# A gated DeltaNet and RWKV-7 decoder block: a rewritten bundle of stages, triangular solves whose joins are held in place, six product steps per RWKV chunk, and the decay products in quarters

## The chip, the cores and the metric

The kernel runs on one core of a Trainium2 chip. The metric is device time in microseconds of one execution, as the median of several. The engines are TensorE (PE in the profile, with its weight loads as PEld), VectorE (DVE), ScalarE (ACT), GpSimd (POOL) and SyncE (SP), which issues the transfers. Each engine runs its instructions in program order; they wait for each other by semaphores.

## The reference

One decoder block on 512 tokens of width 1024, all in float32. In short:

```
mod = silu(c) @ w_ada + b_ada                      # six vectors: shift, scale, gate twice
h   = rms_norm(x) * (1 + scale1) + shift1
p   = h @ w_in                                     # q, k, v, z, gates, the RWKV inputs, ga, gb
q, k, v = silu(causal_conv4(qkv)); q, k l2-normalised per head
# DeltaNet, 8 heads of 64, chunks of 64 tokens:
decay = exp(g_cum[i] - g_cum[j]) for i >= j
T   = inverse(I + strict_lower((beta k) k^T * decay))
o   = chunked recurrence with T, q k^T * decay, state S
y_a = rms_norm(o) * silu(z)
# RWKV-7, 8 heads of 64: S_t = S diag(decay_t) + (S a_t) b_t^T + v_t k_t^T; y_t = S_t r_t
y_b = (group_norm(y) + bonus) * g
x   = x + gate1 * ((sigmoid(ga) * (y_a @ w_bg) + sigmoid(gb) * (y_b @ w_br)) @ w_out)
h   = rms_norm(x) * (1 + scale2) + shift2
x   = x + gate2 * (silu(causal_conv3(h @ w_gate)) * (h @ w_up)) @ w_fo
out = rms_norm(x)
```

The kernel computes the RWKV recurrence in chunks of 64 as well, so both mixers need the inverse of many unit triangular 64x64 matrices (8 heads x 8 chunks each).

## The kernel before, in words

Everything is kept transposed: features on the 128 partitions, the 512 tokens along the free axis. A weight tile of 128 output columns is loaded whole (1024 rows, 512 KB), and split into a high and a low part in fp32r: ACT rounds (whi, L146) and DVE subtracts (wlo, L149). One **step** of a product is three 128x128 by 128x512 matmuls (high x high, high x low, low x high; mm3, L187, L190 and L191), and 8 steps make an output tile of the input projection. The first seven output tiles are made together, one k at a time, straight behind the norm (first_tiles, L310): for each k DVE computes two entries of mod (ada, L202), ACT and DVE make the normalised input (norm_h), and the weights are split on POOL.

All other products stand in a queue. A generator (stream, L232) works it off; fill(n) lets it emit n steps, need(label) lets it run until a product is done. The code between these calls is the rest of the block, and so fill is how steps of products are put into the gaps of the dependent parts. The remaining entries of mod are made by half reductions on DVE (ada_half, L211), some ahead of each product (its late number); their one buffer (wada) is reloaded by SP for each. Instructions are then ordered by a scheduler, which keeps each engine's order free of needless waits by its own estimate; where last["hold"] is set, mm3 gets a dependency on the last small matmul that was emitted through step (L182), so that the products stay where fill put them.

The parts in order:

- first tiles, then convolution and SiLU of q and k, the gates (beta, and the log decay gl, L445 to L478);
- l2 norm of q and k (l2norm, L481), then for each of four groups of two chunks the decay: gt = gl x a triangular mask (POOL, L505), a product with tri_gt (L509), its exponential and mask (DVE, L512), and a product with ones_x (L517) for the total decay eg;
- the chunk products k k^T and q k^T (L622), multiplied by the decay on DVE (L623, L627) and POOL (L624);
- the solve (L541): the 32x32 diagonal blocks are written to a spill buffer (L548) and read back with one matrix per partition (L551), DVE turns and negates them (L552), POOL masks (L553), and 30 elimination steps of two operations (L559, L561) invert them. The inverses go back through two more spill buffers (L563 to L573; ACT turns one copy, L565). After the yield come the joins: four groups of 32 small products (L582, L592) that make the off-diagonal blocks, with ACT's evacuations (L587, L597) between them;
- between the solve and its joins: q and k turned to natural layout (to_natural, L604 and L607), the products of v and the first RWKV inputs, the decay LoRA (L675);
- the DeltaNet scan over 8 chunks (five steps of the stream a chunk, hold set), with the preparation of RWKV among its gaps;
- the RWKV chunk products (L807), the second solve, the output norm (L825) and the first branch product, which the joins of the second solve follow;
- the RWKV scan (L856), 8 steps of the stream a chunk (3, 3 and 2, at L864, L870 and L895);
- group norm, the second branch with the merge (L936), w_out with the residual (L959), and the channel mixer (first_tiles again, L1010, and 37 + 8 products).

Of the kernel before, what the change touches and what calls it, by code (L numbers as in the profile page):

```python
# [18 lines left out]
ALU = mybir.AluOpType  # L19
# [36 lines left out]
def body(ctx, tc, io, out, tap=lambda name, ap: None):  # L56
# [143 lines left out]
    def ada(j, w):  # L200
        sp.dma_start(w, io["w_ada"][j])
# [24 lines left out]
    def product(label, src, xs_, evac, psum=mm, late=0, halves=False, spare=None):  # L226
# [3 lines left out]
        return dict(label=label, pieces=pieces, n=n, xs=xs_, evac=evac, psum=psum, late=late, halves=halves)  # L230

    def stream():  # L232
        while queue:
            it = queue.pop(0)
            for _ in range(min(it["late"], len(ada_rest))):
                ada_half(*ada_rest.pop(0))
# [73 lines left out]
    def first_tiles(src, count, banks, xs_, ready, side, cut=False, behind=()):  # L310
        for k in range(KT):
            ready(k)
            raw = raw_tile()
            sp.dma_start(raw[:, :128 * count].rearrange("p (n j) -> p n j", n=count),
                         src[0:count].rearrange("n p j -> p n j")[:, :, k * 128:(k + 1) * 128])
            hi = wp.tile([128, 1024], F32R, name="whi", tag="whi", bufs=2)
            lo = wp.tile([128, 1024], F32R, name="wlo", tag="wlo", bufs=2)
            split(hi[:, :128 * count], lo[:, :128 * count], raw[:, :128 * count], side if k else dve, () if k else behind)
# [14 lines left out]
    cond = const.tile([128, D], F32, name="cond")  # L333
    table(EXP)
    fn(sc_, cc, AF.Exp, scale=-1.0)
    dve.tensor_scalar(sc_, sc_, 1.0, None, op0=ALU.add)
    dve.reciprocal(sc_, sc_)
    dve.tensor_tensor(sc_, sc_, cc, op=ALU.mult)
    pool.affine_select(out=diag.rearrange("p (k t) -> p k t", k=KT), in_=sc_.unsqueeze(2).broadcast_to([128, KT, 128]),
                       pattern=[[0, KT], [-1, 128]], base=0, channel_multiplier=1, compare_op=ALU.is_equal, fill=0.0)  # L340
    for u in range(2):
        p = pc()
        pe.matmul(p, one, diag[:, T * u:T * u + T], start=True, stop=True)
        act.copy(cond[:, T * u:T * u + T], p)
# [16 lines left out]

    def first_h(k):
        w = slot((2, 3, 8, 9, 12)[k]) if k < 5 else slot2((0, 2, 1)[k - 5])
        ada(8 + k, w[:, 0:D])
        ada(k, w[:, D:2 * D])
        dve.scalar_tensor_tensor(A1[:, k:k + 1], mod[:, 8 + k:9 + k], 1.0, col("norm1", k),
                                 op0=ALU.add, op1=ALU.mult)
        made.append(norm_h(hh[k], hl[k], xT(k), rstd, A1[:, k:k + 1], mod[:, k:k + 1]))

    first_tiles(io["w_in"], 7, first_ps, hx, first_h, pool, behind=whole)  # L370
    sp.dma_start(cons, io["cons"])

    def inproj(t, evac, psum=mm):
        queue.append(product(t, io["w_in"][t], hx, evac, psum, late=2 if t >= T_GB else 2 if t >= T_GA else 0 if t >= T_Z else 0))
# [785 lines left out]
```

## Time and profile before

| what | us |
|---|---|
| median of 3 runs (lowest, highest) | 943.73 (942.07, 944.73) |
| the profiled execution, its own time | 943.86 |
| its span, first to last instruction | 942.2 |
| mean granted TensorE clock | 0.970 |
| first tiles | 16.1 to 65.3 |
| conv, gates, decay, chunk products | 65.3 to 120.7 |
| DeltaNet solve until its joins end | 120.9 to 208.7 |
| DeltaNet scan | 208.7 to 286.3 |
| RWKV chunk products, second solve, its joins | 286.3 to 385.4 |
| RWKV scan | 385.4 to 455.5 |
| group norm | 455.5 to 484.0 |
| merge and w_out | 484.0 to 565 |
| channel mixer | 565 to 942.2 |

The difference of 1.7 between time and span lies around the span. A row of the timeline gives start, duration, engine, line, operation, output <- inputs, shape, and in brackets the idle time before it with what ended it; "xN" means N records in a row. A row of the groups gives count | busy time, mean ns | idle time before it and what ended most of it. L numbers are those of the kernel before.

### The profile page before, as it was taken

The page shows a single profiled execution, that of the slowest core. Times are in us where ns is not written, and L with a number is a line of the kernel's source. Part 1 is how long each engine was busy: PE and PEld are TensorE (multiplying, and loading weights), DVE is VectorE, ACT ScalarE, POOL GpSimd, SP SyncE. Part 2 cuts the span into 40 slices and gives each one's busy share as a digit, 9 for nine tenths or more (in the row PEclk, how much of TensorE's full clock was granted, in tenths as well). Part 3 has the DMA queues.
Part 4 walks back from the last instruction along what each step waited for, and adds up shares of the span by engine and source line. Part 5 has one row for each costly group of instructions (what it writes and reads, how often), then busy time and mean ns, then how long its engine had stood idle before and what let it go on. Part 6 is the DMA issues. An engine that isn't in the chain of part 4 may idle for free.

```text
span 942.2 us, 13945 instructions
## 1 busy us (share of the span) xinstructions
PE 887.0 (94%) x5463; PEld 690.9 (73%) x5463; DVE 548.0 (58%) x865; ACT 413.5 (44%) x663; POOL 150.0 (16%) x126
## 2 busy tenths in 40 slices
PE   5989889989989998899999999999999999999996
PEld 3666566876666776777667788888888888888885
DVE  7988988934976684245568537464544544322233
ACT  5247535355537658323465425343333333332231
POOL 2334630001542100011232230000000000010112
PEclk7999989989999999799999999999999999999998
DMA  9741232473234577444567543332232233533322
GB/s 322 261 151 46 67 101 68 144 170 102 58 90 112 197 232 202 142 146 153 186 200 256 181 139 91 106 106 96 90 103 99 89 105 97 173 101 100 96 89 90
DMA packets 81696, 126.26 MB, mean 134 GB/s; under 512 B 26237, under 2 KB 43005, under 8 KB 81566
## 3 DMA queue, kind: packets, MB, share of 16 engines
q1 hardware_dynamic: 81630, 125.36, 42.4%
q8 instruction: 43, 0.70, 0.3%
q14 instruction: 23, 0.19, 0.1%
HBM read 110.14 MB, written 14.68 MB: 132 GB/s over the span
## 4 chain that ended last, share of the span: by engine, by line
PE 70%; DVE 14%; ACT 7%; DMA 3%; issue 3%; POOL 2%; SPq 0%; DVEq 0%; ACTq 0%; POOLq 0%
PE ps_mm L187 19%; PE ps_mm L191 19%; PE ps_mm L190 19%; PE ps_pc L182 3%; DVE wlo L149 2%; ACT whi L146 1%; DVE slot L202 1%; ACT slot L607 1%; DMA wada<-in_w_ada 1%; DVE slotd L202 1%; DVE wada L211 1%; PE ps_pa L592 1%; ACT tmp_rs L94 1%; PE ps_pc L187 1%; PE ps_pa L622 1%
## 5 line engine op out<-in xcount | busy, mean ns | idle before, releaser
L187 PE MATMUL ps_mm<-hh,whi 128*128 128x512 f32 (+1 forms) x714 | 292.1, 410 | 8.5 <-ACT hh L306 3.5
L191 PE MATMUL ps_mm<-hh,wlo 128*128 128x512 f32 (+1 forms) x714 | 282.5, 396 | 4.7 <-POOL wlo L149 3.5
L190 PE MATMUL ps_mm<-hl,whi 128*128 128x512 f32 (+1 forms) x714 | 282.3, 395 | 1.5 <-DVE hl L307 1.5
L149 DVE TENSOR_TENSOR wlo<-raw,whi 128x1024 fp32r<-128x1024 f32 (+2 forms) x133 | 156.7, 1178 | 169.1 <-ACT whi L146 163.5
L146 ACT CAST whi<-raw 128x1024 fp32r<-128x1024 f32 (+2 forms) x140 | 136.9, 979 | 242.8 <-PE ps_mm L190 190.4
L187 PEld LDWEIGHTS ps_mm<-hh,whi 128*128 128x128 f32 x714 | 136.0, 191 | 47.6 <-issue 9.8
L191 PEld LDWEIGHTS ps_mm<-hh,wlo 128*128 128x128 f32 x714 | 136.6, 191 | 37.9 <-POOL wlo L149 5.2
L190 PEld LDWEIGHTS ps_mm<-hl,whi 128*128 128x128 f32 x714 | 136.7, 191 | 32.1 <-issue 3.6
L191 PE MATMUL ps_mm<-slot,wlo 128*128 128x512 f32 (+1 forms) x154 | 58.5, 380 | 1.7 <-DVE wlo L149 1.7
L187 PE MATMUL ps_mm<-slot,whi 128*128 128x512 f32 (+1 forms) x154 | 58.0, 379 | 0.0
L190 PE MATMUL ps_mm<-slot,whi 128*128 128x512 f32 (+1 forms) x122 | 45.4, 372 | 0.0
L968 POOL COPY tmp_rs<-tmp_sq 128x512 f32<-128x512 f32 x2 | 2.1, 1066 | 268.8 <-ACT tmp_sq L965 268.8
L211 DVE CUSTOM_DVE_ANT_0 wada<-wada,cond,cols 128x512 f32<-128x512 f32 x32 | 25.1, 785 | 26.5 <-DMA wada<-in_w_ada 26.3
L211 DVE CUSTOM_DVE_ANT_0 wada<-wada,cond,half 128x512 f32<-128x512 f32 x32 | 25.2, 787 | 21.7 <-DMA wada<-in_w_ada 21.6
L187 PE MATMUL ps_mm<-slotd,whi 128*128 128x512 f32 (+1 forms) x96 | 36.4, 379 | 0.0
L190 PE MATMUL ps_mm<-slotd,whi 128*128 128x512 f32 (+1 forms) x96 | 36.1, 376 | 0.0
L191 PE MATMUL ps_mm<-slotd,wlo 128*128 128x512 f32 (+1 forms) x96 | 36.1, 376 | 0.0
L970 POOL TENSOR_TENSOR tmp_rs<-tmp_rs,tmp_sq 128x512 f32<-128x512 f32 x12 | 19.5, 1624 | 103.8 <-ACT tmp_sq L965 103.8
L191 PEld LDWEIGHTS ps_mm<-slot,wlo 128*128 128x128 f32 x154 | 29.0, 188 | 9.1 <-DVE wlo L149 4.0
L1035 DVE TENSOR_TENSOR tmp_sg<-tmp_acc,ps_mm 128x512 f32<-128x512 f32 x20 | 13.8, 688 | 35.6 <-PE ps_mm L191 35.5
L385 DVE SCALAR_TENSOR_TENSOR tmp_acc<-ps_mm,cols,tmp_acc 128x511 f32<-128x511 f32 (+2 forms) x44 | 32.8, 745 | 0.7
L187 PEld LDWEIGHTS ps_mm<-slot,whi 128*128 128x128 f32 x154 | 28.9, 188 | 5.8 <-ACT whi L146 0.4
(279 smaller groups left out, 1336.0 us busy)
## 6 DMA issues: line engine op xcount, KB each, us to landing
raw<-in_w_in SPq DMA_DIRECT2D x40, 512.0 KB, 3.5
raw<-in_w_fi SPq DMA_DIRECT2D x37, 512.0 KB, 3.5
wada<-in_w_ada SPq DMA_DIRECT2D x64, 256.0 KB, 3.1
raw<-in_w_fo SPq DMA_DIRECT2D x16, 512.0 KB, 3.5
slot<-in_w_ada SPq DMA_DIRECT2D x10, 512.0 KB, 6.8
slot<-in_xT SPq DMA_DIRECT2D x16, 256.0 KB, 4.1
raw<-in_w_out SPq DMA_DIRECT2D x8, 512.0 KB, 3.7
raw<-in_w_in SPq DMA_DIRECT2D x8, 448.0 KB, 4.5
```

Of the source, the lines that this page charges most:

```text
L94: i = act.activation(*a, **k)
L146: i = act.copy(hi, src)
L149: j = eng.tensor_tensor(lo, src, hi.bitcast(F32), op=ALU.subtract)
L182: last["step"] = pe.matmul(*a, **k)
L187: i = pe.matmul(p, hi, xh, start=start, stop=False)
L190: pe.matmul(p, hi, xl, start=False, stop=False)
L191: pe.matmul(p, lo, xh, start=False, stop=stop)
L202: i = dve.tensor_tensor_reduce(out=w, in0=w, in1=cond, scale=1.0, scalar=col("b_ada", j), op0=ALU.mult, op1=ALU.add, accum_out=mod[:, j:j ...
L211: i = dve.tensor_tensor_reduce(out=w, in0=w, in1=cond[:, part], scale=1.0, scalar=half[:, j:j + 1] if u else col("b_ada", j), op0=ALU.mult ...
L385: dve.scalar_tensor_tensor(acc[:, i:], p[:, :T - i], w[:, taps - 1 - i:taps - i], acc[:, i:], op0=ALU.mult, op1=ALU.add)
L970: pool.tensor_tensor(sums[0], sums[0], sq, op=ALU.add)
L1035: dve.tensor_tensor(t, accs[j], p, op=ALU.mult)
```

## The change

It is a bundle with several parts:

- **First tiles.** The condition is loaded as a row broadcast to all partitions and gets its SiLU by ACT's table, instead of an exponential, a diagonal matrix and two products. Weights and mod rows are fetched a pass ahead; the split's subtraction moves from POOL to DVE, and A1 from DVE to ACT.
- **Conv and l2 norm.** The q tile whose conv was on ACT and POOL (side) now goes through DVE like the others; the l2 norm's square moves from POOL to ACT, and each l2 norm is followed by two steps of the stream instead of one.
- **Decay products.** gt moves to DVE. The two full 128x128 products of each group become four 64x64 quarter products, into two banks that are open together; the lower mask is made by POOL (affine_select) on each half.
- **Chunk products.** POOL's eight 64x256 products become one DVE operation of 64x2048; the scaling of q and k is on DVE; to_natural uses ACT alone for its evacuations.
- **Queue.** The four Z products stand ahead of the V products; the half reductions are 3 ahead of each GA product and 4 ahead of each GB product; the gates get their sigmoid and, for some, the product with the first branch when they are evacuated; two of the GB products are kept until the merge, whose inputs are fetched one product ahead; the merged result goes to other buffers.
- **Held joins.** In the solve, hold is set for the joins and the small products go through step.
- **Six steps.** The RWKV scan has 2, 2 and 2 steps of the stream per chunk.

The core of the diff (the conv, the scaling, the fetching of first tiles and the merge's loads are left out):

```diff
-        pool.tensor_tensor(sq, dst, dst, op=ALU.mult)
+        act.activation(sq, dst, AF.Square)
...
         l2norm(kq[:, 0, j], 1.0)
-        fill(1)
+        fill(2)
         l2norm(kq[:, 1, j], 0.125)
-        fill(1)
+        fill(2)
...
-        pool.tensor_tensor(gt, gl[:, 2 * b:2 * b + 2, :].unsqueeze(3).broadcast_to([128, 2, 4, C]),
+        dve.tensor_tensor(gt, gl[:, 2 * b:2 * b + 2, :].unsqueeze(3).broadcast_to([128, 2, 4, C]),
                            tri_le.unsqueeze(1).unsqueeze(1).broadcast_to([128, 2, 4, C]), op=ALU.mult)
-        p = pa()
-        pe.matmul(p, tri_gt, gtf, start=True, stop=True)
+        p, total_g = pa(), pa()
+        for e in range(2):
+            for q, left, o in ((p, tri_gt, hs(e)), (total_g, ones_x, hs(1 - e))):
+                pe.matmul(q[o], left[hs(e), o], gtf[hs(e)], start=True, stop=True)
...
-        dve.tensor_tensor(ex, ex, mask2[:, 1, :].unsqueeze(1).unsqueeze(1).broadcast_to([128, 2, 4, C]), op=ALU.mult)
+        for e in range(2):
+            d = ex[64 * e:64 * e + 64]
+            pool.affine_select(out=d, in_=d, pattern=[[0, 2], [0, 4], [1, C]], base=0, channel_multiplier=-1,
+                               compare_op=ALU.is_ge, fill=0.0)
...
-        p = pa()
-        pe.matmul(p, ones_x, gtf, start=True, stop=True)
...
         yield
+        held, last["hold"] = last["hold"], True
         for h in range(2):
...
-                    pe.matmul(p[hi_r, i, :], sv[lo_r, 16 * h + i, 32:64], t1[lo_r, 16 * h + i, :],
+                    step(p[hi_r, i, :], sv[lo_r, 16 * h + i, 32:64], t1[lo_r, 16 * h + i, :],
                               start=True, stop=True)
             fill(2)
...
-                    pe.matmul(p[lo_r, i, :], ht[hi_r, i, :], sv[hi_r, 16 * h + i, 32:64],
+                    step(p[lo_r, i, :], ht[hi_r, i, :], sv[hi_r, 16 * h + i, 32:64],
                               start=True, stop=True)
             fill(2)
...
+        last["hold"] = held
...
-        queue.append(product(t, io["w_in"][t], hx, evac, psum, late=2 if t >= T_GB else 2 if t >= T_GA else 0 if t >= T_Z else 0))
+        queue.append(product(t, io["w_in"][t], hx, evac, psum, late=4 if t >= T_GB else 3 if t >= T_GA else 0, begin=begin))
...
+    for j in range(4):
+        inproj(T_Z + j, spill(zsc[j]))
     for j in range(4):
         inproj(T_GV + j, lambda p, j=j: conv(gv[:, j], p, col("conv_gdn", 4 * (8 + j), 4), 4))
...
         act.copy(z, p)
-        fill(3)
+        fill(2)
...
         dve.tensor_scalar(vs[1][hs(1), c], p[hs(1)], -1.0, None, op0=ALU.mult)
-        fill(3)
+        fill(2)
...
-            pool.tensor_tensor(ya_t, sa_t, ya_t, op=ALU.mult)
             dve.tensor_tensor(t, sb_t, p, op=ALU.mult)
-            dve.tensor_tensor(t, t, ya_t, op=ALU.add)
+            sa_t = fetched[("a", n)]
+            if ("a", n) in raw_gate:
+                fn(sa_t, sa_t, AF.Sigmoid)
+            if ("a", n) not in with_y:
+                dve.tensor_tensor(sa_t, sa_t, fetched[("y", n)], op=ALU.mult)
+            dve.tensor_tensor(t, t, sa_t, op=ALU.add)
             split(mh[n], ml[n], t)
```

How the program's order changes at three places. TensorE at the joins of the first solve, before: ps_pa products of 32x32 are the joins, ps_mm rows the steps of the stream; row one ends a step.

```order
L191 MATMUL ps_mm<-hh_113,wlo 128x512
L582 MATMUL ps_pa<-slot_943,slotd_830 32x32 x31
L592 MATMUL ps_pa<-slotd_830,tmp_sg 32x32
L582 MATMUL ps_pa<-slot_943,slotd_830 32x32 x32
L592 MATMUL ps_pa<-slotd_830,tmp_sg 32x32 x63
L182 MATMUL ps_pc<-slot_1206,slotd_830 64x64 x8
L690 MATMUL ps_pa<-slot_473 128x512
```

and after (L619 turns v, L714 is the decay LoRA):

```order
L619 MATMUL ps_pa<-cons,slot_460 128x128 x7
L714 MATMUL ps_pa<-slot_461 128x512 x4
L181 MATMUL ps_pa<-slot_965,slotd_859 32x32 x32
L186 MATMUL ps_mm<-hh_110,whi 128x512
L189 MATMUL ps_mm<-hl_118,whi 128x512
L190 MATMUL ps_mm<-hh_110,wlo 128x512
L186 MATMUL ps_mm<-hh_111,whi 128x512
L189 MATMUL ps_mm<-hl_119,whi 128x512
L190 MATMUL ps_mm<-hh_111,wlo 128x512
L181 MATMUL ps_pa<-slotd_859,tmp_sg 32x32 x32
```

Before, the joins stand behind 184 steps of the stream, without steps among them, and the scan (L182, ps_pc) is right behind them. After, they stand behind 158 steps and the decay LoRA, with two steps behind each group; 52 more steps follow them ahead of the scan.

DVE at the start of the first solve's elimination, before: L385 is the conv of v, L552 the turn of the blocks that came back, L559 and L561 the elimination.

```order
L385 SCALAR_TENSOR_TENSOR slot_472<-ps_mm,cols,slot_472 128x511
L385 SCALAR_TENSOR_TENSOR slot_472<-ps_mm,cols,slot_472 128x510
L149 TENSOR_TENSOR wlo<-raw,whi 128x1024
L385 SCALAR_TENSOR_TENSOR slot_472<-ps_mm,cols,slot_472 128x509
L552 TENSOR_SCALAR slot_943<-slot_943 128x1024
L211 ISA wada,mod<-wada,cond,half 128x512
```

and after (L398 is the conv, L565 the turn, L572 and L574 the elimination):

```order
L148 TENSOR_TENSOR wlo<-raw,whi 128x1024
L565 TENSOR_SCALAR slot_965<-slot_965 128x1024
L572 TENSOR_TENSOR pr<-slot_965 128x30
L574 TENSOR_TENSOR slot_965<-slot_965,pr 128x30
L572 TENSOR_TENSOR pr<-slot_965 128x58
L574 TENSOR_TENSOR slot_965<-slot_965,pr 128x29x2
L572 TENSOR_TENSOR pr<-slot_965 128x84
L209 ISA wada,half<-wada,cond,cols 128x512
```

Nine of twelve conv operations of v stood ahead of the turn before; now all twelve stand among the elimination, with nine half reductions.

TensorE at the decay products, before:

```order
L509 MATMUL ps_pa<-tmp_acc,cons 128x512
L517 MATMUL ps_pa<-tmp_acc,cons 128x512
L190 MATMUL ps_mm<-hl_114,whi 128x512
L191 MATMUL ps_mm<-hh_106,wlo 128x512
L509 MATMUL ps_pa<-tmp_acc,cons 128x512
```

and after:

```order
L524 MATMUL ps_pa<-tmp_acc,cons 64x512 x2
L186 MATMUL ps_mm<-hh_107,whi 128x512
L189 MATMUL ps_mm<-hl_115,whi 128x512
L190 MATMUL ps_mm<-hh_107,wlo 128x512
L186 MATMUL ps_mm<-hh_108,whi 128x512
L524 MATMUL ps_pa<-tmp_acc,cons 64x512 x6
```

The quarter products come in runs of two, six, four and four, with steps of the stream between the runs.

More of the change, by code (lines that the diff above doesn't have):

```diff
@@ L224, in body, with product @@
     queue, done = [], set()
-    def product(label, src, xs_, evac, psum=mm, late=0, halves=False, spare=None):
+    def product(label, src, xs_, evac, psum=mm, late=0, halves=False, spare=None, begin=None, ahead=0):
         n = src.shape[-1] // 128
@@ L229, in product @@
                   for k0 in range(0, n, 8)]
-        return dict(label=label, pieces=pieces, n=n, xs=xs_, evac=evac, psum=psum, late=late, halves=halves)
+        return dict(label=label, pieces=pieces, n=n, xs=xs_, evac=evac, psum=psum, late=late, halves=halves, begin=begin, ahead=ahead)
     def stream():
@@ L234, in stream @@
             it = queue.pop(0)
+            for nx in [it] + queue[:it["ahead"]]:
+                if nx["begin"] is not None:
+                    nx["begin"]()
+                    nx["begin"] = None
             for _ in range(min(it["late"], len(ada_rest))):
@@ L308, in norm_h, with first_tiles, fetch @@
         return i
-    def first_tiles(src, count, banks, xs_, ready, side, cut=False, behind=()):
+    def first_tiles(src, count, banks, xs_, ready, load, cut=False, behind=()):
+        raws = []
+        def fetch(k):
+            if k < KT:
+                load(k)
+                raws.append(raw_tile())
+                sp.dma_start(raws[k][:, :128 * count].rearrange("p (n j) -> p n j", n=count),
+                             src[0:count].rearrange("n p j -> p n j")[:, :, k * 128:(k + 1) * 128])
+        for k in range(2):
+            fetch(k)
         for k in range(KT):
+            if k:
+                fetch(k + 1)
             ready(k)
-            raw = raw_tile()
-            sp.dma_start(raw[:, :128 * count].rearrange("p (n j) -> p n j", n=count),
-                         src[0:count].rearrange("n p j -> p n j")[:, :, k * 128:(k + 1) * 128])
+            raw = raws[k]
             hi = wp.tile([128, 1024], F32R, name="whi", tag="whi", bufs=2)
             lo = wp.tile([128, 1024], F32R, name="wlo", tag="wlo", bufs=2)
-            split(hi[:, :128 * count], lo[:, :128 * count], raw[:, :128 * count], side if k else dve, () if k else behind)
+            split(hi[:, :128 * count], lo[:, :128 * count], raw[:, :128 * count], dve, () if k else behind)
             if k == 0 and cut:
@@ L331, in first_tiles @@
                 mm3(banks[i], (blocks(hi), blocks(lo)), i, xs_[k], k == 0, k == KT - 1)
-    cond = const.tile([128, D], F32, name="cond")
+    table(SILU)
+    fn(cond, cond, AF.Silu)
     table(EXP)
[L335 to L344, printed above, removed]
     total = tmp("rs")
@@ L488, in l2norm, with hs @@
         dve.scalar_tensor_tensor(dst, dst, scale, rs, op0=ALU.mult, op1=ALU.mult)
+    def hs(e):
+        return slice(64 * e, 64 * e + 64)
     eg = ct4(slot(3))
@@ L647, in body @@
     rr_ = ar[:, 1]
-    zsc = dr.tile([4, 128, T], F32, name="zsc")
     ysc = dr.tile([KT, 128, T], F32, name="ysc")
@@ L661, in body, with fetch, f, gate @@
         shift_in(T_RV + j, rv_[:, j], 8 + j)
-    for j in range(4):
-        inproj(T_Z + j, spill(zsc[j]))
+    sig_in = [False]
+    raw_gate, with_y = set(), set()
+    fetched = {}
+    def fetch(label, tag, src):
+        def f():
+            fetched[label] = tmp(tag)
+            sp.dma_start(fetched[label], src)
+        return f
+    def gate(n, dst):
+        def f(p):
+            o = tmp("sp")
+            if sig_in[0]:
+                fn(o, p, AF.Sigmoid)
+            else:
+                act.copy(o, p)
+                raw_gate.add(n)
+            if ("y", n) in fetched:
+                dve.tensor_tensor(o, o, fetched.pop(("y", n)), op=ALU.mult)
+                with_y.add(n)
+            sp.dma_start(dst, o)
+        return f
     for n in range(KT):
-        inproj(T_GA + n, spill(asc[n]))
-    for n in range(KT):
-        inproj(T_GB + n, spill(bsc[n]))
+        inproj(T_GA + n, gate(("a", n), asc[n]),
+               begin=lambda n=n: fetch(("y", ("a", n)), "rs", ysc[n])() if ("bg", n) in done else None)
+    for n in range(KT - 2):
+        inproj(T_GB + n, gate(("b", n), bsc[n]))
     lw = ct4(slot(12))
@@ L838, in body @@
         split(ga_h[ct], ga_l[ct], sg)
+    table(SIG)
+    sig_in[0] = True
     gx = list(zip(ga_h, ga_l))
@@ L951, in body @@
     for n in range(KT):
-        queue.append(product(("br", n), io["w_br"][n], bx, merge(n), late=2))
+        if n in (0, 3):
+            g = KT - 2 + n // 3
+            queue.append(product(T_GB + g, io["w_in"][T_GB + g], hx, last_gate(g), ahead=1))
+        queue.append(product(("br", n), io["w_br"][n], bx, merge(n), begin=merge_in(n), ahead=1))
     x2s = [slot(9), slot(3)]
```

96 lines of the change are left out of this document (55 added, 41 removed).

## The prediction

> **What bounds the kernel now.** I read the page for the span, then the table by stage, cut at the program's own joints.
>
> ```profile
> span 942.2 us, 13945 instructions
> ...
> 16.10:65.30 49.20, 43.87 (x170) 32.82 (x171) 44.83 (x57) 16.22 (x21) 16.07 (x8) 0.95 0.71 241
> 124.80:201.50 76.70, 70.89 (x298) 55.12 (x296) 61.10 (x128) 32.48 (x47) 8.65 (x5) 0.96 0.47 130
> 201.50:208.70 7.20, 5.83 (x256) 5.54 (x256) 0.51 (x1) 3.92 (x7) 0.00 (x0) 0.78 0.37 141
> 208.70:286.30 77.60, 72.51 (x668) 48.81 (x667) 53.15 (x84) 41.12 (x80) 27.31 (x26) 0.93 0.28 86
> 385.40:455.50 70.10, 70.10 (x777) 53.77 (x775) 33.64 (x64) 22.71 (x42) 6.20 (x7) 0.97 0.47 153
> 484.00:565.00 81.00, 77.44 (x338) 62.24 (x337) 46.47 (x63) 37.67 (x55) 22.80 (x15) 0.98 0.61 201
> ```
>
> After the stretch come its length and the busy time of PE, PEld, DVE, ACT and POOL, then PE's clock. TensorE is busy nearly everywhere, so a change pays only where it removes TensorE work or a wait of TensorE, and costs where it adds a wait. DVE is the fuller engine only in the first stretch (44.83 of 49.20). The unit of the sum is one step of the product stream, three 128x512 matmuls:
>
> ```profile
> 193.12 0.39 PE L187 MATMUL ps_mm<-hh,whi 128*128 128x512 f32 x1
> 193.80 0.39 PE L187 MATMUL ps_mm<-hh,whi 128*128 128x512 f32 x1
> ```
>
> One step is 0.68 us. The number of steps is the same before and after; what moves is where TensorE has none to run. That is decided by the first triangular solve, whose chain is this (columns: start, duration):
>
> ```profile
> 120.90 0.86 DVE L627 TENSOR_TENSOR slotd<-ps_pa,slotd 64x256 f32<-64x256 f32 x2
> 136.58 0.33 SPq L551 DMA_DIRECT2D slot<-lsc_g  x1
> 144.16 1.53 DVE L385 SCALAR_TENSOR_TENSOR slot<-ps_mm,cols,slot 128x511 f32<-128x511 f32 x2 [5.93 <-ACT slot L383]
> 150.36 0.19 DVE L559 TENSOR_TENSOR pr<-slot 128x30 f32<-128x30 f32 x1 [1.16 <-POOL slot L553]
> 189.31 2.11 ACT L565 COPY pr<-slot 128x1024 f32<-128x1024 f32 x1 [4.09 <-DVE slot L561]
> 196.17 1.27 SPq L573 DMA_DIRECT2D slot<-tsc_g  x1
> 201.53 1.19 PE L582 MATMUL ps_pa<-slot,slotd 32*32 32x32 f32 x62 [1.03 <-DMA slot<-tsc_g]
> 208.66 0.58 PE L182 MATMUL ps_pc<-slot,slotd 64*64 64x64 f32 x6
> ```
>
> The matrices are complete at 121.8 (call it T0). The elimination runs on DVE from T0 + 28.6 to T0 + 67.5; copy, writes and reads add 12.2; the join starts at T0 + 79.7 after a wait of only 1.0 us, and takes 7.1. TensorE is covered because the scheduler put its waiting work, 180 steps by then in the order, ahead of the join. The change fixes that place by hand.
>
> **Part by part.** *First tiles.* What paces them is DVE:
>
> ```profile
> 17.04 1.28 DVE L202 CUSTOM_DVE_ANT_0 slot<-slot,cond,cols 128x1024 f32<-128x1024 f32 x1
> 19.45 2.04 DVE L366 SCALAR_TENSOR_TENSOR A<-mod,cols 128x1 f32<-128x1 f32 x1
> 25.27 2.07 DVE L366 SCALAR_TENSOR_TENSOR A<-mod,cols 128x1 f32<-128x1 f32 x1
> L149 POOL TENSOR_TENSOR wlo<-raw,whi 128x896 fp32r<-128x896 f32 x7 | 15.5, 2221 | 31.9 <-ACT whi L146 28.3 <-DMA raw<-in_w_in 3.6
> L149 DVE TENSOR_TENSOR wlo<-raw,whi 128x1024 fp32r<-128x1024 f32 x9 | 11.0, 1220 | 0.1
> ```
>
> A pass takes 25.27 - 19.45 = 5.82. One-element L366 lasts 2 us because it sits beside POOL's split. New DVE work of a pass: two reductions of 1.2 (the pipelined spacing), two norm operations of 0.67, one split of 896 columns at 1220 x 7/8 = 1.07: 4.8. Seven passes give -7.0; SiLU of the condition on ACT, now ahead of the norm, takes back about 1.8 (an estimate: ACT's copy of the same width takes 2.11 in L565). Term: -5.2, bounds -8 and 0, since the DMA share is already 0.71.
>
> *To T0.* The four ones_x products go into the shadow of the tri_gt ones:
>
> ```profile
> 97.84 1.10 PE L509 MATMUL ps_pa<-tmp_acc,cons 128*128 128x512 f32 x2 [0.22 <-POOL tmp_acc L505]
> 98.77 1.02 PE L517 MATMUL ps_pa<-tmp_acc,cons 128*128 128x512 f32 x2
> 286.80 0.28 PE L807 MATMUL ps_pc<-slotd,slot 64*64 64x128 f32 x2
> 286.81 0.33 PE L807 MATMUL ps_pa<-slotd,slot 64*64 64x128 f32 x2
> PE ps_pa L509 <- POOL tmp_acc L505: 1.8, 2, 1.6
> PE ps_pa L622 <- DVE slotd L627: 1.8, 1, 1.8
> ```
>
> A full product starts 0.93 after the last. Quarter products in two banks begin 0.01 apart in L807, so four quarters should cost what one full product does: -4 x 0.93 = -3.7 (in turn they would cost four times 0.93 a group instead of twice: +7.4). The two waits quoted go with POOL's work: -2.1 of 3.6 (0 to -3.6). POOL gets the decay mask instead, two halves a group beside DVE and TensorE; its nearest rows are 128x512 operations of 1 to 2.2 us, so it could give 2 of this back, and I leave it inside the bound. The new order runs seven more steps here (two per l2norm): +4.8. So T0 moves by -5.2 - 3.7 - 2.1 + 4.8 = -6.2, to 115.6. A rule speaks against this part: the Trainium skill, "TensorEngine Tiling (Array Packing)", Key Properties, says that a change of tiling mode drains TensorE. [...]
>
> *The first join.* In the new order the conv operations of DVE (L385, held to 147 by the products) stand behind the solve's start, so the 5.93 idle before them goes: start at T0 + 22.7. The read of the spilled blocks (L551) now stands on SP behind two spills of Z products and one weight load; the second of those products is 14 steps and a set of transposes (4.1) behind T0, so it is issued at about T0 + 14, as before at T0 + 14.8. Then DVE is in order: 60 eliminations, and by the order 9 half reductions, 12 conv operations and 5 splits among them.
>
> ```profile
> L561 DVE TENSOR_TENSOR slot<-slot,pr 128x30 f32<-128x30 f32 (+14 forms) x30 | 9.9, 330 | 0.5
> L559 DVE TENSOR_TENSOR pr<-slot 128x30 f32<-128x30 f32 (+14 forms) x30 | 9.8, 327 | 1.8 <-POOL slot L553 1.2
> L211 DVE CUSTOM_DVE_ANT_0 wada<-wada,cond,half 128x512 f32<-128x512 f32 x5 | 3.7, 747 | 1.7 <-DMA wada<-in_w_ada 1.7
> ```
>
> 19.7 + 9 x 0.75 + 12 x 0.7 + 5 x 1.14 = 40.5, against 38.9 before. With the same 12.2 the join can start at T0 + 75.4 = 191.0. TensorE gets there after 60 steps, the second set of transposes and the gate products: before, 124.80:201.50 held about 90 steps (298 records with the rest) in 76.7, so 30 fewer at 0.68 leave 56: at about 171. It stands 20 us before a join with 52 steps queued behind it in program order, which it may not run; ACT and DVE have nothing to evacuate meanwhile, and SP's weight loads stop at full buffers. Then four groups of 1.8 and 58 steps: 191.0 + 7.2 + 39.6 = 237.8 for the scan's start, and 1.5 for a clock that falls during the wait (0 to 3: 201.50:208.70 ran at 0.78). 239.3 against 208.66: +30.6, with 32 steps (21.8) more behind it: 9 net, the 20 us wait less the 10.5 won earlier. On the clock, the Trainium skill, "TensorE: Matmul & The Clock Gate", Part 1, gives half rate after about one idle window of 3.4 us and one busy window to return; an estimate from that is 1.7 us lost at each held join.
>
> *DeltaNet scan:* the same order; it started at half clock (0.93 on the mean) and may not: -2 (0 to -4).
>
> *Second join and RWKV scan:*
>
> ```profile
> 321.93 0.18 DVE L559 TENSOR_TENSOR pr<-slot 128x30 f32<-128x30 f32 x1
> 360.30 2.11 ACT L565 COPY pr<-slot 128x1024 f32<-128x1024 f32 x1
> 376.54 0.63 PE L582 MATMUL ps_pa<-slot,slotd 32*32 32x32 f32 x28
> 404.91 0.68 PE L182 MATMUL ps_pc<-cz,slotd 64*64 64x64 f32 x16
> 406.05 0.43 DVE L869 TENSOR_SCALAR slotd<-ps_pc 64x256 f32<-64x256 f32 x1 [0.42 <-ACT slot L868]
> ```
>
> The second elimination took 38; in the new order it holds 10 splits and 6 half reductions, 32, so it ends 6 sooner and the join can start 12 after it, at 366 on the old axis, where TensorE waits since about 357. Four groups and 8 steps: to 379; the scan of 48 steps instead of 61 from the join's end: 70.1 - 14 x 0.68 = 60.6, plus 3 for evacuations that two steps (1.4) do not cover. A product's results are stored 0.9 after its end (404.91 + 0.68 to 406.48), so alone they fit; half reductions that wait for their DMA stand between. Ends at 442.5 against 455.5: -13 (-16 to -8).
>
> *Merge:* its TensorE waits are
>
> ```profile
> PE ps_mm L191 <- DVE wlo L149: 2.2, 3, 1.2
> PE ps_mm L187 <- ACT whi L146: 1.4, 1, 1.4
> ```
>
> and the half clock behind them; 112 steps (338 records) take 76.4 of the 81.0. Loading early, without POOL, can win at most 4.6: -4 (-4.6 to 0). The gates' sigmoid and their product with the first branch move into evacuations up to the RWKV scan: one DVE product of 0.69 each, beside TensorE. The channel mixer is unchanged: 0.
>
> **Sum.** The profiled execution took 943.86: 942.2 and 1.7 around it, 0.1 above the median of 943.73. +30.6 - 2 - 13 - 4 = +11.6: 955.5, rounded 956.
>
> **Rivals.** *The solves arrive in time (faster).* If the elimination were not interleaved as counted, or the spills landed sooner, so that the first join is ready when TensorE is (171, that is T0 + 55 instead of T0 + 75), the waits of 20 and 9 vanish: 927. It turns to faster once the two waits together shrink by more than 12. For it: DVE's dependent steps are short and much of DVE's work between them could slip. Against: DVE runs in order, and 19.7 + 12.2 alone is 32 of the 55. 0.17. *Half of it:* waits shorter by 6 and 3, or the first stages gain their lower bounds: 945, no change. 0.10. *Quarters run in turn:* +7.4 instead of -3.7 ahead of T0, 967; L807 speaks against. 0.07. *Six steps expose the evacuations:* 16 gaps lose 0.5 more each, +8: 964. DVE's waits for the half reductions speak for it. 0.10. *Not as said:* the order shows the join held, so no chance.
>
> **How the numbers follow.** The forecast has 0.56. A measurement here tells apart about 0.3%, 2.8 us. Slower takes the forecast and the two dear rivals, less the part of the forecast's spread that reaches 946: 0.70; faster the first rival and a part of the second: 0.22; same 0.08. Range: low 938, between the early solve and the half, high 968, a dear rival with the upper bounds of clock and scan.
>
> **What would show it.** Right: TensorE waiting 15 to 25 us ahead of the first small 32x32 products for the read-back DMA, scan start near 239, a second wait near 9, passes of 4.9 us in the first tiles, the scan's chunks near 7.7. Wrong: no wait longer than 5 us there; first-tile passes still near 5.8; or quarter products in a row instead of side by side.

## The result, and the profile after

| | us |
|---|---|
| before, median of 4 runs (lowest, highest) | 944.23 (942.07, 944.96) |
| changed, median of 4 runs (lowest, highest) | 954.79 (951.61, 955.55) |
| ratio, with its 95% interval | 1.0104 [1.0075, 1.0132] |
| profiled execution of the changed kernel, its own time | 955.55 |
| its span | 953.8 (before 942.2) |
| mean granted TensorE clock | 0.971 (before 0.970) |

The kernel became 1% slower, 10.6 us by the medians and 11.6 by the spans. The forecast was 956 (938 to 968), slower at 0.70.

The page and the table by stage of the changed kernel, cut at its own joints. The columns are those of the table shown of before.

```profile
span 953.8 us, 13900 instructions
...
19.70:71.60 51.90, 51.87 (x216) 42.41 (x216) 48.34 (x70) 25.25 (x39) 0.52 (x1) 1.00 0.67 228
118.20:190.00 71.80, 57.58 (x256) 41.98 (x254) 52.56 (x120) 31.93 (x58) 3.17 (x3) 0.88 0.46 142
190.00:242.00 52.00, 46.96 (x430) 38.27 (x430) 21.03 (x36) 16.97 (x24) 0.00 (x0) 0.91 0.47 133
242.00:315.90 73.90, 68.05 (x668) 45.90 (x667) 54.05 (x87) 40.81 (x79) 28.01 (x26) 1.00 0.34 105
411.40:471.50 60.10, 58.96 (x701) 44.03 (x696) 28.73 (x53) 18.62 (x37) 5.82 (x6) 1.00 0.40 129
502.40:576.80 74.40, 74.19 (x338) 61.68 (x337) 42.19 (x57) 31.33 (x43) 10.86 (x7) 1.00 0.55 176
```

Every other stage shown is denser or shorter than before. The exception is the first solve with its joins (rows two and three): in row two TensorE idles for 14.2 of 71.8 us (before 5.8 of 76.7), and its clock falls to 0.88. A ledger between events that both kernels have shows the rest. The steps of the stream are counted in TensorE's rows; step 395 lies in the merge, step 500 at its end.

| stretch | before | after | change | forecast |
|---|---|---|---|---|
| to the first product of the DeltaNet scan | 208.7 | 242.1 | +33.4 | +30.6 |
| first to last product of the DeltaNet scan | 75.2 | 71.4 | -3.8 | -2 |
| from there to the last product of the RWKV scan | 170.2 | 160.2 | -10.0 | -13 |
| from there to step 395 (group norm) | 32.3 | 31.2 | -1.1 | 0 |
| step 395 to step 500 (merge) | 77.2 | 70.1 | -7.1 | -4 |
| step 500 to the end (channel mixer) | 378.6 | 378.8 | +0.2 | 0 |
| sum | 942.2 | 953.8 | +11.6 | +11.6 |

At the scan's start the changed kernel has 216 steps behind it and the old one 184. The 32 more are worth 21.8 us at 0.68 a step. At step 395, where both have the same steps behind them, the changed kernel is 18.5 us late (504.9 against 486.4): that is the loss, and it stands ahead of the merge. The merge then wins 7.1 of it back.

The timeline of the changed kernel through the first solve (start, duration; idle time before it and its releaser in brackets):

```profile
121.66 0.86 DVE L642 TENSOR_TENSOR slotd<-ps_pa,slotd 64x256 f32<-64x256 f32 x2
135.23 0.32 SPq L564 DMA_DIRECT2D slot<-lsc_g  x1
143.85 0.19 DVE L572 TENSOR_TENSOR pr<-slot 128x30 f32<-128x30 f32 x1 [1.43 <-POOL slot L566]
170.12 0.63 ACT L94 ACTIVATE slot<-slot 128x512 f32<-128x512 f32 x1 [3.44 <-DVE slot L398]
173.62 0.65 PE L619 MATMUL ps_pa<-cons,slot 128*128 128x128 f32 x4 [2.27 <-ACT slot L622]
175.19 6.96 PE L714 MATMUL ps_pa<-slot 65*128 65x512 f32 x8 [0.92 <-issue]
182.87 0.19 DVE L574 TENSOR_TENSOR slot<-slot,pr 128x30 f32<-128x30 f32 x1
190.04 0.28 PE L181 MATMUL ps_pa<-slot,slotd 32*32 32x32 f32 x2 [7.88 <-issue]
195.33 1.91 PE L181 MATMUL ps_pa<-slot,slotd 32*32 32x32 f32 x62 [5.01 <-DMA slot<-tsc_g]
242.08 0.68 PE L181 MATMUL ps_pc<-slot,slotd 64*64 64x64 f32 x16
183.00:195.30 12.30, 0.28 (x2) 0.18 (x2) 1.58 (x5) 1.95 (x1) 0.00 (x0) 0.50 0.87 207
```

The matrices are complete at T0 = 122.5 (before 121.8). The elimination starts 21.3 later and lasts 39.2, and the join starts 12.3 behind it, at 195.3. TensorE is done with the decay LoRA (L714) at 182 and then has nothing that it may run. The last row is the table by stage for that wait: 0.28 us of work in 12.3, at half clock. The profile can put 5.01 of it down to the read-back DMA; the 7.88 ahead of it carry only "issue", in front of two products of the same join. Ahead of that TensorE waits for the transposes of v: its conv stands among the elimination on DVE (L398), ACT waits 3.44 for it and TensorE for ACT.

### The profile page after: what moved, and what is told of

Its sections match the earlier page's. It is cut to its first block, busy times and chain, and to the rows that moved or that the text cites. A ratio compares the mean times of both kernels' runs of the same rounds, so it can differ in the third digit from the quotient of the medians.

```text
span 953.8 us, 13900 instructions
## 1 busy us (share of the span) xinstructions
PE 880.5 (92%) x5475; PEld 687.3 (72%) x5475; DVE 536.8 (56%) x866; ACT 416.4 (44%) x672; POOL 95.0 (10%) x91
## 4 chain that ended last, share of the span: by engine, by line
PE 68%; DVE 13%; DMA 8%; issue 4%; ACT 4%; POOL 1%; SPq 1%; DVEq 0%; POOLq 0%; ACTq 0%
PE ps_mm L186 19%; PE ps_mm L189 18%; PE ps_mm L190 18%; DMA wada<-in_w_ada 7%; DVE wlo L148 2%; DVE wada L209 2%; PE ps_pc L181 2%; DVE slot L574 1%; PE ps_pa L181 1%; DVE pr L572 1%; PE ps_pc L186 1%; PE ps_pc L190 1%; PE ps_pc L189 1%; PE ps_pa L186 1%; PE ps_pa L189 1%
## 5 line engine op out<-in xcount | busy, mean ns | idle before, releaser
L186 PE MATMUL ps_mm<-hh,whi 128*128 128x512 f32 (+1 forms) x642 | 263.6, 411 | 8.1 <-ACT hh L308 3.4
L190 PE MATMUL ps_mm<-hh,wlo 128*128 128x512 f32 (+1 forms) x642 | 254.5, 398 | 0.6 <-DVE wlo L148 0.5
L189 PE MATMUL ps_mm<-hl,whi 128*128 128x512 f32 (+1 forms) x642 | 253.5, 395 | 0.0
L190 PEld LDWEIGHTS ps_mm<-hh,wlo 128*128 128x128 f32 x642 | 122.1, 190 | 30.7 <-issue 3.7
L189 PEld LDWEIGHTS ps_mm<-hl,whi 128*128 128x128 f32 x642 | 122.5, 191 | 25.9 <-issue 2.9
L186 PE MATMUL ps_mm<-slot,whi 128*128 128x512 f32 (+1 forms) x226 | 85.1, 377 | 3.7 <-ACT tmp_sp L94 3.7
L190 PE MATMUL ps_mm<-slot,wlo 128*128 128x512 f32 (+1 forms) x226 | 85.3, 377 | 1.9 <-DVE wlo L148 1.9
L189 PE MATMUL ps_mm<-slotd,whi 128*128 128x512 f32 (+1 forms) x168 | 62.4, 371 | 0.0
L186 PEld LDWEIGHTS ps_mm<-slot,whi 128*128 128x128 f32 x226 | 43.0, 190 | 11.5 <-ACT tmp_sp L94 3.9
L190 PEld LDWEIGHTS ps_mm<-slot,wlo 128*128 128x128 f32 x226 | 42.8, 190 | 10.9 <-DVE wlo L148 3.5
L189 PE MATMUL ps_mm<-slot,whi 128*128 128x512 f32 (+1 forms) x122 | 45.3, 372 | 0.0
L186 PE MATMUL ps_mm<-slotd,whi 128*128 128x512 f32 (+1 forms) x96 | 36.4, 380 | 0.0
L189 PEld LDWEIGHTS ps_mm<-slotd,whi 128*128 128x128 f32 x168 | 31.6, 188 | 5.6
L398 DVE SCALAR_TENSOR_TENSOR tmp_acc<-ps_mm,cols,tmp_acc 128x511 f32<-128x511 f32 (+2 forms) x44 | 32.8, 746 | 0.7
```

The source lines that it names most:

```text
L186: i = pe.matmul(p, hi, xh, start=start, stop=False)
L189: pe.matmul(p, hi, xl, start=False, stop=False)
L190: pe.matmul(p, lo, xh, start=False, stop=stop)
L398: dve.scalar_tensor_tensor(acc[:, i:], p[:, :T - i], w[:, taps - 1 - i:taps - i], acc[:, i:], op0=ALU.mult, op1=ALU.add)
```

## The experiments

**Theory A.** The loss is TensorE's idle time at the first held join: the join is pinned to a place that TensorE reaches before the inverses are back, and the 42 or more steps that follow it may not be moved ahead. Freed, or pinned later, the kernel loses nothing there, and the rest of the bundle is a gain. **Theory B.** The hold costs little, since steps not run ahead of a join are run behind it; the rest of the bundle loses the time: half reductions on DVE, quarter products, six steps a chunk.

Each comparison is with the kernel before on the same chip, whose medians were 945.79, 945.84 and 945.89 for the three groups (e1 to e4, e5 to e8, e9 to e12).

### Free joins, in both solves and in the first alone

The changed kernel, with the joins as free as the code around them is (e1), and held in the second solve alone (e2):

```diff
-        held, last["hold"] = last["hold"], True
+        held, last["hold"] = last["hold"], last["hold"]    # e1
+        held, last["hold"] = last["hold"], name == "r"     # e2
```

> The changed kernel with the joins of both solves no longer held (their small products still go through step). Theory A (TensorE idles at the held joins): the first join moves behind 187 steps of the stream, the wait of 12.9 us ahead of it and the idle around it go; the scan starts about 213 with 200 steps done instead of 242 with 216, which is 18 us less for the same work; about 937 (933 to 942). Theory B (the hold is harmless since the same steps run behind it, and the loss comes from the rest of the bundle, chiefly the half reductions that wait for their reload ahead of the scan): within 3 us of 954.8.

> The changed kernel with the hold taken from the joins of the first solve only. Theory A: nearly all of the loss is at the first solve, so 17 to 18 us less than the changed kernel, about 937; the second hold costs 1 to 2. If the two holds share the loss, about 946. Theory B: 954.8 within 3.

Measured: e1 936.11 (931.52 to 937.11), ratio 0.9894 [0.9853, 0.9934]; e2 938.38, ratio 0.9917 [0.9886, 0.9948]. In e1's timeline the join and the scan, and its table by stage ahead of the join:

```profile
206.44 1.19 PE L181 MATMUL ps_pa<-slot,slotd 32*32 32x32 f32 x62
212.88 1.12 PE L181 MATMUL ps_pc<-slot,slotd 64*64 64x64 f32 x16
188.00:206.40 18.40, 18.40 (x82) 14.70 (x80) 6.03 (x14) 5.97 (x6) 0.00 (x0) 1.00 0.83 215
```

The join starts 11 us later than in the changed kernel, and the scan 29 us earlier, with 200 steps done instead of 216. TensorE is busy in all 18.4 us ahead of the join, at full clock. 29.2 less 16 steps (10.9) is 18.3, and the span is 18.4 shorter. Not all of the 18.4 is there yet when the DeltaNet scan ends: with 252 steps done in both, its last product comes at 299.1 instead of 313.5, 14.4 sooner. The other 4 come between there and the end of the RWKV scan, a stretch that took 160.2 in one profile of the changed kernel and 155.7 in another (e5). In e1 step 395 comes at 486.4, as in the kernel before, and the merge takes 70.1 against 77.2; so by these two profiles what the rest of the bundle wins is the merge. Both intervals lie clear of the changed kernel's, and e2 is within e1's: nearly everything comes from freeing the first solve's joins.

### The hold alone, and the hold at a later place

The kernel before with nothing but the held joins (e3):

```diff
         yield
+        held, last["hold"] = last["hold"], True
...
-                    pe.matmul(p[hi_r, i, :], sv[lo_r, 16 * h + i, 32:64], t1[lo_r, 16 * h + i, :],
+                    step(p[hi_r, i, :], sv[lo_r, 16 * h + i, 32:64], t1[lo_r, 16 * h + i, :],
...
-                    pe.matmul(p[lo_r, i, :], ht[hi_r, i, :], sv[hi_r, 16 * h + i, 32:64],
+                    step(p[lo_r, i, :], ht[hi_r, i, :], sv[hi_r, 16 * h + i, 32:64],
...
+        last["hold"] = held
```

> The kernel before with the hold put on its joins and nothing else. By the order the first join then stands behind 126 steps instead of 180, and 58 steps come between it and the scan. Theory A: TensorE arrives at about 162 for a join that is ready at 201, and the scan starts near 248 instead of 209 with the same 184 steps done: 980 (970 to 988), more than the changed kernel loses, since the Z products are not ahead of the join. Theory B: 944 to 948.

Measured: 972.37 (967.86 to 976.26), ratio 1.0285 [1.0234, 1.0336]. TensorE's rows in e3 (there the scan's and the joins' small products are L182):

```profile
190.50 0.28 PE L182 MATMUL ps_pa<-slot,slotd 32*32 32x32 f32 x2 [21.46 <-DMA slot<-tsc_g]
194.06 1.91 PE L182 MATMUL ps_pa<-slot,slotd 32*32 32x32 f32 x62 [3.29 <-DMA slot<-tsc_g]
243.30 0.68 PE L182 MATMUL ps_pc<-slot,slotd 64*64 64x64 f32 x16
```

Without the rest of the bundle only 126 steps stand ahead of the join, TensorE waits 24.8 us for it, and the scan starts at 243.3 with the same 184 steps as before (208.7). The dose goes with the wait: 12.9 us of it in the changed kernel, 24.8 here.

Is it the hold, or its place? In e12 the joins of the changed kernel stay held, but the products up to the last RWKV input are emitted ahead of them:

```diff
+    need(T_RR + 3)
     for _ in gsolve:
         pass
-    need(T_RR + 3)
```

> The changed kernel with both joins still held, but the call that runs the remaining joins of the first solve stands behind the need for the last r product instead of ahead of it; by the order the first join then stands behind 200 steps. Theory A (the hold costs by its place, not by itself): no wait over 3 us ahead of the first join, 13 to 18 less than the changed kernel, 934 to 940. If the hold itself (steps bound to the last small product) costs: within 5 of 952.

Measured: 939.10, ratio 0.9932 [0.9903, 0.9962]. In e12's timeline the join's first row has no idle time in front:

```profile
206.84 1.20 PE L181 MATMUL ps_pa<-slot,slotd 32*32 32x32 f32 x64
```

200 steps are done by then, and the scan starts at 216.6. A held join that stands where TensorE arrives after the inverses do costs nothing that these runs resolve: the medians of e12 and e1, 939.10 and 936.11, have overlapping intervals.

### The quarter products

The changed kernel with full products again, into the same two banks (e4), the changed kernel unchanged a second time (e5), e4 with free joins (e6), and the quarter products alone in the kernel before (e8):

```diff
-        for e in range(2):
-            for q, left, o in ((p, tri_gt, hs(e)), (total_g, ones_x, hs(1 - e))):
-                pe.matmul(q[o], left[hs(e), o], gtf[hs(e)], start=True, stop=True)
+        for q, left in ((p, tri_gt), (total_g, ones_x)):          # e4, e6
+            pe.matmul(q, left, gtf, start=True, stop=True)
...
-        p = pa()
-        pe.matmul(p, tri_gt, gtf, start=True, stop=True)
+        p, total_g = pa(), pa()                                   # e8
+        for e in range(2):
+            for q, left, o in ((p, tri_gt, hs(e)), (total_g, ones_x, hs(1 - e))):
+                pe.matmul(q[o], left[hs(e), o], gtf[hs(e)], start=True, stop=True)
```

> The changed kernel with the decay products as two full 128x128 products per group again, into the same two banks. If four quarters take the time of one full product: 4 groups times 0.93 us later, and the first join as much later: 958.5 (957 to 960). If the quarters ran in turn: faster than the changed kernel, about 947 to 951. If other work hides it: 954.8 within 1.5.

> The changed kernel as it is, beside the kernels of this call. The full decay products came out 5 to 6 us faster than the quarters, but on another chip than the changed kernel. If that was the chip: within 2 of 949.4. If it is the quarters: again 1.010 of the kernel before, about 955.

> Free joins (as e1) and full decay products (as e4). Theory C (quarters leave TensorE idle in a stretch that DVE and ACT pace, so its clock falls to half, and the chunk products behind them run later): 3 to 5 us less than e1, about 932. Theory D (the quarters save 4 times 0.93 us of TensorE's time, and the gain of e4 hangs on the held join): 3 to 4 us more than e1, about 939.5. Hidden in both: within 1.5 of e1.

> The kernel before with the decay products as four quarters into two banks and nothing else; its masks and POOL's products stay. Theory D: 3 to 4 us less than before, 0.996. Theory C, or DVE and POOL pace this stretch: no gain, 0.998 to 1.003.

Measured:

| | median | ratio | T0 |
|---|---|---|---|
| e5, changed (quarters) | 952.12 | 1.0064 [1.0040, 1.0088] | 120.9 |
| e4, changed, full | 949.42 | 1.0041 [1.0019, 1.0062] | 120.4 |
| e1, free joins, quarters | 936.11 | 0.9894 [0.9853, 0.9934] | 121.0 |
| e6, free joins, full | 937.02 | 0.9909 [0.9878, 0.9941] | 119.7 |
| e8, before with quarters | 947.11 | 1.0013 [0.9989, 1.0037] | 124.3 |

Repeated on another chip, the changed kernel is slower by 0.6% instead of 1.0%, with overlapping intervals. No pair of quarters and full products differs beyond its intervals, and T0 comes no sooner with quarters in any of them (before: 121.8). The median of e4 is where its expectation put quarters that run in turn; its rows below exclude that. Yet the group itself became shorter. First a group's row in the changed kernel and the table over its chunk products, then the same two in e4 (L523 is the decay product there):

```profile
104.64 1.09 PE L524 MATMUL ps_pa<-tmp_acc,cons 64*64 64x512 f32 x8
107.20:121.20 14.00, 11.91 (x136) 9.27 (x135) 12.49 (x25) 3.02 (x4) 1.33 (x3) 0.88 0.12 39
```

```profile
104.46 1.88 PE L523 MATMUL ps_pa<-tmp_acc,cons 128*128 128x512 f32 x4
107.70:118.80 11.10, 10.23 (x136) 7.98 (x135) 10.88 (x23) 2.63 (x4) 2.39 (x2) 1.00 0.15 49
```

Eight quarter records take 1.09 us where four full ones take 1.88. What is won there is gone at the next stage: the same 136 records of the chunk products take 14.0 us at a clock of 0.88 instead of 11.1 at 1.00. DVE is the fuller engine in both (12.49 of 14.0, 10.88 of 11.1). TensorE's wait for DVE ahead of the fourth chunk, in the changed kernel, in e4, and in e9 of the next section:

```profile
112.95 3.11 PE L638 MATMUL ps_pa<-slotd 64*64 64x128 f32 x32 [1.98 <-DVE slotd L642]
```

```profile
112.13 2.29 PE L637 MATMUL ps_pa<-slotd 64*64 64x128 f32 x32 [0.75 <-DVE slotd L641]
```

```profile
110.08 2.29 PE L638 MATMUL ps_pa<-slotd 64*64 64x128 f32 x32 [1.13 <-DVE slotd L642]
```

In the changed kernel the granted clock is 0.50 from 114.3 to 117.7 behind that wait, and DVE, which was the later one, then waits for TensorE (0.69 us at 118.3). The other runs fit: ten profiles, before's among them, have a wait of 1.78 or more in this stretch and a clock of 0.87 to 0.89 over it; in the four with 1.13 or less (e4, e6, e9, e10) it stays at 1.00.

### The half reductions behind the chunk products

If DVE paces the stretch, taking work off DVE there must move T0. In e9 the next half reduction, and so those queued behind it, is placed behind the scaling of q and k, which moves five of them out of the stretch; e10 is e9 with e1's free joins:

```diff
-            dve.tensor_tensor(qs[e][q, :, tc_], p[q, :, 1], ee[q, c], op=ALU.mult)
+            last["gate"] = dve.tensor_tensor(qs[e][q, :, tc_], p[q, :, 1], ee[q, c], op=ALU.mult)
```

> The changed kernel (joins held) with the first half reduction placed behind the last chunk product, so that none stands among the decay and the chunk products on DVE. Theory E (DVE paces that stretch, which is why the shorter products did not bring the solve forward): five reductions of 0.75 and about 1.1 of reload waits leave it, T0 comes 3 to 5 earlier and with it the first join and the scan; 3 to 4 less than the changed kernel (948 to 949 where that has 952). Rival: the reloads, 3.6 apart, only move to the stretch behind the join, where they already hold the scan's first DVE operation; no gain, or up to 15 more. If TensorE paces the stretch: T0 unmoved.

> As the last, with the joins free (e1). Theory E with the joins free: the first join is not waited for, so an earlier T0 is worth only TensorE's own idle time in the stretch, 0 to 3 less than e1 (0.986 to 0.990 of before). Rival: the moved reloads delay the scan, 2 to 8 more than e1.

Measured: e9 948.35, ratio 1.0030 [1.0004, 1.0057]; e10 934.64 (932.40 to 935.41), ratio 0.9885 [0.9850, 0.9919]. One of the five in the changed kernel's timeline, and then, in e9's, the last row of the chunk products on DVE and the table over them:

```profile
107.47 1.08 DVE L209 CUSTOM_DVE_ANT_0 wada<-wada,cond,cols 128x512 f32<-128x512 f32 x1 [0.68 <-DMA wada<-in_w_ada]
```

```profile
117.50 0.86 DVE L642 TENSOR_TENSOR slotd<-ps_pa,slotd 64x256 f32<-64x256 f32 x2
105.80:119.00 13.20, 11.90 (x141) 9.11 (x137) 12.41 (x27) 3.75 (x8) 4.33 (x4) 1.00 0.11 29
```

T0 is 118.4 in e9 and 118.7 in e10, against 120.9 and 121.0 without the move: 2.3 to 2.5 us sooner, and the clock stays at 1.00 with quarter products in place. So the quarters don't lower the clock by themselves. The total follows by 3.8 (e5 to e9) with held joins and by 1.5 (e1 to e10) with free ones; the intervals overlap in both pairs, so that a gain is likely and not proven. T0 itself scatters: six profiles whose code up to there is the changed kernel's (its own and those of e1, e2, e5, e7 and e12) have it from 120.0 to 122.5. What does not scatter is the stretch from the first chunk product to T0: 15.0 to 15.3 in these six, 13.1 in e9 and e10, 12.8 and 12.9 with full products (e4, e6). e10, the lowest median of the study, beats before by 1.15% and the changed kernel by 1.8% (934.64 against e5's 952.12 on the same chip).

### Six steps or eight a chunk

e7 is e1 with the RWKV scan's 3, 3 and 2 steps again, e11 the kernel before with 2, 2 and 2:

```diff
-        fill(2)
+        fill(3)      # e7, twice; e11 the reverse
```

> Free joins (as e1) and eight steps per chunk of the RWKV scan again (3, 3, 2). In the changed kernel's scan most chunks take 7.7 where those of before take 9.05, which is just the two steps; two chunks are 1.1 and 0.5 longer. If six steps only move steps out of the scan: within 2 of e1, 0 to 1.6 less. If six steps expose the evacuations as my rival had it: 6 to 8 less than e1. If eight steps make the scan wait: 3 more.

> The kernel before with 2, 2 and 2 steps in the RWKV scan and nothing else. If six steps only move steps out of the scan: within 2 of before (0.998 to 1.002). If evacuations are exposed: 6 to 8 more.

Measured: e7 940.28, ratio 0.9945 [0.9917, 0.9972], against e1's 0.9894 [0.9853, 0.9934]; e11 950.17, ratio 1.0037 [1.0004, 1.0069]. Eight steps are some 4 us dearer inside the bundle, where the expectation was 0 to 1.6 cheaper or 3 dearer; the intervals overlap, and by the profiles there is no difference (spans of 935.3 and 935.4). In the kernel before, six steps are dearer by 0 to 0.7%. So six steps are no gain by themselves; whether the bundle turns them into one stays open.

## Why the prediction was right

The mechanism was the one forecast, and theory A held: TensorE waits at a join that was pinned ahead of its data, while steps that it could run stand behind. That the total of 956 comes so close to 954.8 is luck: it is better than its parts, several of which missed in opposite directions. At step 395 the changed kernel is 18.5 late where the terms up to there add up to 15.6, and the merge wins 3 more than its term. Of the signs named, a wait of 15 to 25 us (it was 12.9) and a second wait near 9 did not come.

**First tiles: right.** The pass of 4.8 us, in the changed kernel's timeline (the norm's product with A, one pass apart):

```profile
22.91 0.74 DVE L307 SCALAR_TENSOR_TENSOR tmp_acc<-slot,A,tmp_rs 128x512 f32<-128x512 f32 x1
27.65 0.74 DVE L307 SCALAR_TENSOR_TENSOR tmp_acc<-slot,A,tmp_rs 128x512 f32<-128x512 f32 x1
```

4.74, and the stream reaches step 72 at 72.7 instead of 77.5: -4.8 where the term was -5.2. The first product itself starts 3.6 later (19.7 against 16.1), twice the 1.8 estimated for the condition's SiLU.

**To T0: the step that failed.** T0 was forecast at 115.6, 6.2 sooner, and came at 122.5, 0.8 later (in six profiles of the same code up to there, 120.0 to 122.5). Of its four terms the first tiles arrived and the seven steps (+4.8) were run; the -3.7 of the quarter products and the -2.1 of POOL's waits did not arrive. The row-level part was right: quarters run side by side, as L807 had them. What failed is the inference that a shorter TensorE group moves T0. The last decay product ends at 105.7 instead of 107.3, and the first chunk product starts at 107.2 in both kernels. The sum to T0 left out DVE, for which the chunk products then wait 1.98 us, and the half clock behind that wait. The change puts gt, the wide product and five half reductions on DVE; e9 takes only these last away, its wait is 1.13 without a half clock, and T0 comes 2.3 to 2.5 sooner. Where the rest of the missing 5.8 went is not shown. The rule of the Trainium skill, "TensorEngine Tiling (Array Packing)", Key Properties, that a change of tiling mode drains TensorE, spoke against this part. No run isolates the drain; since a whole group is down from 1.88 to 1.09, it can't be what ate the 3.7.

**Elimination and read-back: right.** Start at T0 + 21.3 (forecast 22.7), 39.2 long (40.5), 12.3 behind it (12.2).

**TensorE's arrival: wrong by 11, and it cancelled the error in T0.** Forecast 171, measured 182. The sum took all steps at 0.68 and left out that the transposes of v stand behind conv operations that DVE runs between its eliminations, and that the eight records of the decay LoRA would run at half clock: 7.0 us where they were busy for 4.0 before. With T0 seven late and the arrival eleven late, the wait at the join was 12.9 instead of 20, and the rest of TensorE's idle time, some 6 us, sat in front of it. For the sum it doesn't matter where TensorE idles ahead of a pinned join: the join came at 195.3 (191.0), the scan at 242.1 (239.3).

**The clock behind the wait: right.** Four rows of TensorE behind the join, in the changed kernel:

```profile
197.17 0.80 PE L186 MATMUL ps_mm<-hh,whi 128*128 128x512 f32 x1
199.86 1.20 PE L181 MATMUL ps_pa<-slotd,tmp_sg 32*32 32x32 f32 x64
200.99 0.50 PE L186 MATMUL ps_mm<-hh,whi 128*128 128x512 f32 x1
202.58 1.20 PE L181 MATMUL ps_pa<-slot,slotd 32*32 32x32 f32 x64
```

The two steps behind the first group take 2.69 us (197.17 to 199.86), the two behind the second 1.59, and the first group's 62 products 1.91 against 1.19 in e1: 1.1 and 0.7, so 1.8 lost within some 4.5 us. The sum had 1.5. The Trainium skill, "TensorE: Matmul & The Clock Gate", Part 1, from which 1.7 was worked out, agrees with this trace behind the join: 0.50 during the wait and up to 199.6, 4.3 us behind the join's start, and 1.00 from there on. It does not agree ahead of the wait: from 176 to 182 the decay LoRA's records follow each other without a gap, and the clock stays at 0.50. Nor did it take an idle window of 3.4 us to fall: the wait of 1.98 us was enough among the chunk products.

**DeltaNet scan: right in sign** (-3.8, forecast -2). It runs at 1.00 on the mean where it ran at 0.93.

**Second join and RWKV scan: right in kind, too large by 3.** The second elimination lasts 32.2 (forecast 32). The 3 lie ahead of the second join's end: -3.5 against -6.4. Behind it the scan gave -6.5, as forecast, but by two errors: the sum subtracted 14 steps where TensorE's rows give 10 fewer (49 against 59 up to the last product), and added 3 for evacuations of which 0.3 came. The wait of 9 us ahead of the second join didn't come as one; TensorE, in the changed kernel's timeline, came late by waits for ACT:

```profile
395.68 0.66 PE L619 MATMUL ps_pa<-cons,slot 128*128 128x128 f32 x4 [1.64 <-ACT slot L622]
397.21 1.70 PE L181 MATMUL ps_pa<-slot,slotd 32*32 32x32 f32 x64 [0.88 <-ACT slot L622]
421.24 0.68 PE L181 MATMUL ps_pc<-cz,slotd 64*64 64x64 f32 x16
428.93 0.68 PE L181 MATMUL ps_pc<-cz,slotd 64*64 64x64 f32 x16
```

The rows show waits for ACT's to_natural copies (L622) where the wait for the inverses was forecast. It isn't the change that put these on ACT: the copies to natural layout ahead of the second join were all ACT's before, and one of the three tensors is now shared with DVE. Only the copies of k and v in the first solve went to ACT alone. The scan's chunk is 7.69, as said.

**Merge: a term too small.** -7.1 against -4, below a bound of -4.6. The bound took 112 steps at 0.68, 76.4 us; the 338 records take 74.2, 0.66 a step. The stage is dense now (74.19 of 74.40), so the direction was right, and TensorE's waits for the split weights are gone from this stage; no run tests which part of the change removed them.

**The rivals.** The early solve did not happen: the inverses were back no sooner than counted. Quarters in turn: excluded by the row of 1.09. Six steps exposing the evacuations: the chunk of 7.69 speaks against its +8. The half of the waits was the nearest miss, as the wait at the join was shorter by 7, but only because TensorE came later.

## What to carry to other kernels

A dependency that pins a waiting product into an in-order queue is safe only where the engine arrives after the data does; look up both times at that place, and let it be moved later, or free, if the data is late. It isn't the work behind the join that is lost but the time until it starts: waits of 12.9 and 24.8 us at this join against none 42 steps further on. Before you count a saving on one engine, look which engine the next event of the chain waits for; here the next products waited for DVE, and a TensorE group that was 40% shorter bought nothing.

## What the runs showed of the hardware that was not expected

Less TensorE work did not mean a shorter stage: with the clock at 0.88 instead of 1.00, the same 136 records took 11.91 us of TensorE's time instead of 10.23 (the changed kernel and e4, above). In nine profiles a wait of 1.78 to 1.98 us in that stretch was followed by half clock for 3.4 us; in the four with a wait of 0.75 to 1.13 us there was none. In between nothing was measured.

Gapless work did not always bring the clock back: the decay LoRA's eight records (65 rows by 512) ran at 0.50 throughout in five profiles (the changed kernel, e3, e4, e5 and e9), one behind the other for about 7 us. Why was not tested.

A load into a single buffer can pace DVE. In the changed kernel's timeline, at the first chunks of the DeltaNet scan:

```profile
247.31 0.75 DVE L209 CUSTOM_DVE_ANT_0 wada<-wada,cond,half 128x512 f32<-128x512 f32 x1 [1.12 <-DMA wada<-in_w_ada]
250.89 0.76 DVE L209 CUSTOM_DVE_ANT_0 wada<-wada,cond,cols 128x512 f32<-128x512 f32 x1 [2.82 <-DMA wada<-in_w_ada]
252.04 0.68 PE L181 MATMUL ps_pc<-cz,slotd 64*64 64x64 f32 x16 [0.35 <-DVE cz L788]
```

The half reductions stand in front of the chunk's own operation on DVE, and each waits for the reload of their one buffer; the scan's next products start behind them. A second buffer was not tried.
